# Retention's output product by seven block products over both halves of the contraction, with block sums made in DRAM by accumulating DMAs and the gate applied at the end

## The chip, the cores and the metric

The kernel runs on one core of one Trainium2 chip. The core has a matrix engine (TensorE, PE in the profile), three engines for elementwise work (VectorE or DVE, ScalarE or ACT, GpSimd or POOL), a queue engine that here only issues DMAs (SyncE or SP), and 16 DMA engines, shared by all queues. The metric is device time in microseconds (us), the median of several runs. Each engine executes its own instructions strictly in the order in which the program emits them; engines are tied together by semaphores alone.

## The reference, cut to what matters

One decoder block, 1024 tokens by 1024 channels, all in float32. The part in question ends the retention branch:

```python
ro = (ro * gn_g + gn_b)                        # normalized heads, (S, 2048)
ret_out = (silu(rg) * ro) @ w_ret_out          # (S, 2048) @ (2048, 1024)
...
att_out = att @ w_att_out                      # (S, 512) @ (512, 1024)
merged = sigmoid(gate_a) * ret_out + sigmoid(gate_b) * att_out
x = x + g1 * (merged @ w_o)
```

Call `u = silu(rg) * ro` the gated head output; `ret_out` is a product with a contraction of 2048.

## The kernel before, in words

Activations lie transposed, channels on the 128 partitions and the 1024 tokens in the free dimension. Full precision comes from splitting each operand into a rounded part ("high", type fp32r) and the remainder ("low"): ScalarE copies the high part, VectorE subtracts to get the low part, and `mm3` (L191 to L199) issues three matmuls for each product of a 128x128 weight block with 512 tokens: low weight by high data (L195), high by low (L197), high by high (L199). So 128x128 by 512 tokens costs three PE instructions everywhere.

The stages, in order of time: the startup (loads of `x`, of the adaLN weights `w_ada` and of the first value weights, L377 to L418 and `av_first`, L774), the attention values (`av_step`, L849), the queries, keys and gates by seven block products (`queries_keys`, L934, class `Blocks`, L214), four retention heads (`v_first` L605, `v_rest` L621, `chunk` L670), the attention pairs (`att_step` L1326, `cover_step` L1360, `gate_step` L1410), the two output products, `w_o` (`wo_step`, L1540), and the MLP (`ff1`, `ff2_blocks`, `ff2`, `ff2_last`).

Seven block products are Winograd's form of Strassen's scheme: a product split in 2x2 blocks is made by seven products of sums of blocks in place of eight. The kernel uses it already for queries, keys and gates, for the first MLP product and for a part of the second.

The order of work is written out by hand. `Steps` (L55 to L130) runs a list of steps; each has weights (and other tiles) to load into a ring of three buffers `raw`, which SP issues ahead, and a preparation (the split) that is emitted one or two steps before the body that uses it. A step marked `manual` calls `ahead` itself at the place where the next step's preparation is to be emitted.

Around the change:

- `u_final` (L661) ends a retention head: ScalarE scales and shifts a 128x1024 tile `on` (L665), VectorE multiplies it by the silu of the gate (L667), SP stores it as `u` in DRAM (L668). That of the last head is emitted inside the first attention step (L1344).
- `att_out_step` (L1468) makes 192 matmuls in four steps (tiles `ao` in PSUM) and multiplies the gate of the attention branch, kept in SBUF as `G[1, i]` (tag `g1`), by the result (L1483). It also loads the eight tiles of the retention gate (`gate_load(0, i)`, L1474).
- `ret_out_step` (L1486), 16 steps of 48 matmuls: for each head `h` and output pair `j`, four 128-row slices of `u` (split by `u_prep`, L1444) by the weights `w_ret_out`. VectorE multiplies each PSUM result by the gate (L1495), and GpSimd, or for the last head VectorE, adds it to `G[1, i]` (L1496). With the last head the sum is split into `mh` and `ml` (L1502, L1503), 128x512 tiles from a ring of 32 buffers with tag `mh`, the operand of `w_o`.
- `wo_step` makes two halves of 512 tokens by eight outputs, 24 matmuls each.

GpSimd's own order: one small power for the first norm (L356), eight DMAs near the end of `queries_keys` that bring back the second halves of the normalized input (L950, L951), small jobs in the retention heads (L561, L720), nothing in attention, the adds at L1496, and adds for the later norms (L1538).

Of the kernel before, what the change touches and what calls it, by code (L numbers as in the profile page):

```python
# [11 lines left out]
F32 = mybir.dt.float32  # L12
# [5 lines left out]
P = 128  # L18
D = 1024
S = 1024  # L20
# [34 lines left out]
class Steps:  # L55
# [16 lines left out]
    def run(self, pre):  # L72
# [42 lines left out]
        for s, (loads, body, manual) in enumerate(self.steps):  # L115
            prepare(s, len(loads))
            mine = weights_of(s)
            args = [r for r in results[s] if r is not None]
            if manual:
                body(lambda room=3 - mine, only=False: prepare(s + 1, room, only), *args)  # L120
            else:
                room = 3 - max(mine, 1)
                for t in (s + 1, s + 2):
                    if t < len(self.steps) and room > 0:
                        done = sum(getattr(p, "weight", False) for _, p in self.steps[t][0][:len(results[t])])
                        prepare(t, room - done, t == s + 2)
                        room -= weights_of(t)
                        if len(results[t]) < len(self.steps[t][0]):
                            break
                body(*args)  # L130

@with_exitstack
def block_kernel(ctx, tc, io, stop=None, dbg=None):
# [385 lines left out]
    u_d = [dram.tile([P, S], F32, name=f"u{i}") for i in range(16)]  # L519
# [141 lines left out]
    def u_final(h, es=range(4)):  # L661
        for e in es:
            i = h * 4 + e
            t = hd["on"][e]
            nc.scalar.activation(t, t, AF.Identity, scale=vec[:, VC_GNG + i:VC_GNG + i + 1],  # L665
                                 bias=vec[:, VC_GNB + i:VC_GNB + i + 1])
            nc.vector.tensor_mul(t, t, hd["srg"][e])  # L667
            nc.sync.dma_start(u_d[i], t)  # L668
# [265 lines left out]
    def queries_keys(ahead):  # L934
        sums_of_h("t4")
# [390 lines left out]
    def att_step(pair, i):  # L1326
# [3 lines left out]
        def body(*args):  # L1330
# [7 lines left out]
            elif pair == 0:  # L1338
# [5 lines left out]
                u_final(H - 1)  # L1344
                open_att()
# [98 lines left out]
    def u_prep(h, e):  # L1444
        def prep(raw):
            if h % 2 == 0:
                r = []
                for j in range(2):
                    s = raw[:, 512 * j:512 * j + 512]
                    hi, lo = mh(f"uh{h}{e}{j}"), mh(f"ul{h}{e}{j}")  # L1450
                    nc.scalar.copy(hi, s)
                    nc.vector.tensor_sub(lo, s, fv(hi))
                    r.append((hi, lo))
            else:
                hi = A["r1"].tile([P, S], F32R, tag="att", bufs=8, name=f"uh{h}{e}")
                lo = A["r1"].tile([P, S], F32R, tag="att", bufs=8, name=f"ul{h}{e}")
                nc.scalar.copy(hi, raw)
                nc.vector.tensor_sub(lo, raw, fv(hi))
                r = halves(hi, lo)
            G["u", h, e] = r  # L1460
        return prep

# [5 lines left out]
    def att_out_step(j):  # L1468
        def body(w):
            xs = [halves(*A["att", h]) for h in range(4)]  # L1470
            for i in (2 * j, 2 * j + 1):
                if j < 2:
                    gate_load(1, i + 4)
                gate_load(0, i)  # L1474
# [9 lines left out]
        return body  # L1484

    def ret_out_step(h, j):  # L1486
        def body(w):
            xs = [G["u", h, e] for e in range(4)]
            for f in range(2):
                i = 2 * j + f  # L1490
                ps = ps_mm(f"ro{h}{j}{f}")
                k4_mm(ps, w, f, xs)
                m, sg = G[1, i], G[0, i]
                t = G["mp"].tile([P, S], F32, tag="rl", bufs=2, name=f"rt{h}{i}")
                nc.vector.tensor_mul(t, flat(ps), sg)  # L1495
                (nc.vector if h == H - 1 else nc.gpsimd).tensor_add(m, m, t)  # L1496
                if h == H - 1:
                    r = []
                    for hf in range(2):
                        s = m[:, 512 * hf:512 * hf + 512]  # L1500
                        hi, lo = mh(f"mh{i}{hf}"), mh(f"ml{i}{hf}")
                        nc.scalar.copy(hi, s)  # L1502
                        nc.vector.tensor_sub(lo, s, fv(hi))  # L1503
                        r.append((hi, lo))
                    G["m", i] = r
            if h == H - 1 and j > 0:
                x1_load(2 * j - 2)
                x1_load(2 * j - 1)
        return body


    behind = []
    for j in range(4):
        steps.add(att_out_step(j), [wsplit(io["w_att_out"][j])] + behind)
        behind = [(u_d[j], u_prep(0, j))]
    for h in range(H):
        for j in range(4):
            steps.add(ret_out_step(h, j), [wsplit(io["w_ret_out"][4 * h + j])] + behind)
            behind = [(u_d[4 * (h + 1) + j], u_prep(h + 1, j))] if h + 1 < H else []
# [20 lines left out]
    def wo_step(hf, f):  # L1540
        def body(w):
            if hf == 0 and f == 0:
                x1_load(6)
                x1_load(7)
# [8 lines left out]
            for k in range(NK):  # L1553
                mm3([ps], wk(w, k), [G["m", k][hf]], k == 0, k == NK - 1)
# [128 lines left out]
    def ff1(ahead):  # L1683
# [7 lines left out]
        banks(True)  # L1691
# [383 lines left out]

def _vcols(w, width):
# [45 lines left out]
def pack(x, c, w_ada, b_ada, norm1_g, w_in, rel_bias, ret_gn_g, ret_gn_b,  # L2122
# [23 lines left out]
        "w_ret_out": _k4(A(w_ret_out)[0]),  # L2146
# [25 lines left out]
```

## Time and profile before

| | us |
|---|---|
| median of 3 runs | 2281.12 |
| lowest and highest run | 2278.60 and 2281.48 |
| the profiled execution, whole | 2279.53 |
| its span, first to last instruction | 2277.7 |
| PE busy within the span | 2223.6 (98%) |
| VectorE, ScalarE, GpSimd busy | 1444.6, 848.5, 171.4 |

The span of the profiled execution is 1.8 us shorter than its device time; the rest lies before the first and after the last instruction. The granted TensorE clock was 0.997. Rows of the profile give an engine, a source line, an operation, "written <- read" by the program's names, a count, and times. "Idle before" is the time in which the engine stood still ahead of an instruction, with what released it. PE's matmuls overlap in the pipe, so one matmul's duration is longer than the distance to the next.

### The profile page before, as it was taken

The numbers are of one execution on the slowest core, as the hardware profiler recorded it, in microseconds if no ns is written. First come the engines' busy times: TensorE is split into PE (matmuls) and PEld (weight loads), VectorE is DVE, ScalarE is ACT, GpSimd is POOL, SyncE is SP. The second block draws the span as 40 slices with busy tenths as digits, with TensorE's granted clock in tenths as the row PEclk, the third lists the DMA queues.
The fourth block names the chain that finished last, engine by engine and source line by source line (L and its number), as shares of the span: only waits on it lengthen the run. The fifth ranks groups of instructions, "written<-read, shape, count | busy, mean of one in ns | idle before, by whom it ended". The sixth has DMA issues, their size and how long they took to land.

```text
span 2277.7 us, 26769 instructions
## 1 busy us (share of the span) xinstructions
PE 2223.6 (98%) x10322; PEld 1837.4 (81%) x10322; DVE 1444.6 (63%) x2149; ACT 848.5 (37%) x1557; POOL 171.4 (8%) x136
## 2 busy tenths in 40 slices
PE   7999999999999999999999999999999999999998
PEld 5887888888878787888788788888777788788887
DVE  6526555546767687764554646666876665787845
ACT  4333233212334343344534522124454444433412
POOL 0000000001101020100000004501100000000003
PEclk9999999999999999999999999999999999999999
DMA  9533333333323223233323353335134443754322
GB/s 360 198 122 111 111 112 111 111 123 117 121 84 121 93 84 136 68 132 94 103 77 103 103 203 93 99 106 200 60 141 153 153 152 111 271 174 167 120 84 74
DMA packets 112317, 293.53 MB, mean 129 GB/s; under 512 B 23094, under 2 KB 34621, under 8 KB 112062
## 3 DMA queue, kind: packets, MB, share of 16 engines
q1 hardware_dynamic: 111038, 289.72, 36.7%
q0 software_dynamic: 1152, 2.10, 0.3%
q8 instruction: 81, 1.33, 0.2%
q14 instruction: 46, 0.38, 0.0%
HBM read 217.70 MB, written 76.44 MB: 129 GB/s over the span
## 4 chain that ended last, share of the span: by engine, by line
PE 45%; DVE 9%; ACT 4%; issue 2%; DMA 1%; POOL 0%; SPq 0%; POOLq 0%; DVEq 0%; ACTq 0%
PE ro L195 3%; PE ro L197 3%; PE ro L199 3%; PE fp L195 2%; PE fp L197 2%; PE fp L199 2%; PE ak L195 2%; PE ak L197 2%; PE ak L199 2%; PE f2a L197 2%; PE f2a L199 2%; PE f2a L195 2%; PE f2c L199 1%; PE f2c L195 1%; PE f2c L197 1%
## 5 line engine op out<-in xcount | busy, mean ns | idle before, releaser
L1496 POOL TENSOR_TENSOR g<-g,rt 128x1024 f32<-128x1024 f32 x24 | 66.1, 2754 | 431.3 <-DVE rt L1495 431.3
L195 PE MATMUL qap<-hh,qaw 128*128 128x512 f32 x216 | 84.3, 390 | 2.5 <-DVE qat L279 1.7
L199 PE MATMUL qap<-hh,qaw 128*128 128x512 f32 x216 | 84.1, 389 | 0.0
L197 PE MATMUL qap<-hl,qaw 128*128 128x512 f32 x216 | 84.0, 389 | 0.0
L1495 DVE TENSOR_TENSOR rt<-ro,g 128x1024 f32<-128x1024 f32 x32 | 39.0, 1219 | 56.4 <-PE ro L199 44.2
L561 POOL TENSOR_TENSOR j<-qk,j 128x512 fp32r<-128x512 f32 x32 | 43.8, 1370 | 364.4 <-ACT j L560 364.4
L1538 POOL TENSOR_TENSOR accnf<-accnf,sqnf 128x256 f32<-128x256 f32 (+1 forms) x18 | 16.6, 920 | 624.9 <-ACT sqnf L1537 624.9
L1640 ACT ACTIVATE a<-a 128x512 f32<-128x512 f32 x48 | 30.3, 632 | 84.9 <-DVE a L1639 84.9
L252 DVE TENSOR_TENSOR qaw<-wa,qaw 128x512 fp32r<-128x512 f32 x54 | 36.7, 690 | 39.5 <-ACT qaw L242 39.5
L1126 ACT ACTIVATE P<-P,ng 128x128 f32<-128x128 f32 (+1 forms) x96 | 41.9, 439 | 40.2 <-DVE ng L1123 40.2
L252 DVE TENSOR_TENSOR fw<-w1r,fw 128x512 fp32r<-128x512 f32 x48 | 33.0, 688 | 37.5 <-ACT fw L242 37.5
L639 ACT CAST vh<-v 128x512 fp32r<-128x512 f32 x32 | 18.8, 587 | 89.1 <-PE v L603 82.7
L1825 ACT CAST w2h<-w2s 128x512 fp32r<-128x512 f32 x36 | 22.4, 621 | 78.7 <-DVE w2s L1863 78.7
L581 ACT COPY sm<-sT 128x128 f32<-128x128 f32 x32 | 8.5, 266 | 114.1 <-PE sT L572 114.1
L195 PEld LDWEIGHTS qap<-hh,qaw 128*128 128x128 f32 x216 | 40.5, 188 | 11.7 <-DVE qat L279 2.1
L195 PE MATMUL fp<-h2h,fw 128*128 128x512 f32 x128 | 50.0, 390 | 0.0
L199 PE MATMUL fp<-h2h,fw 128*128 128x512 f32 x128 | 49.8, 389 | 0.0
L197 PE MATMUL fp<-h2l,fw 128*128 128x512 f32 x128 | 49.8, 389 | 0.0
L199 PEld LDWEIGHTS qap<-hh,qaw 128*128 128x128 f32 x216 | 40.5, 188 | 8.5
L197 PEld LDWEIGHTS qap<-hl,qaw 128*128 128x128 f32 x216 | 40.5, 188 | 8.3
L242 ACT CAST qaw<-wa 128x512 fp32r<-128x512 f32 x54 | 32.5, 617 | 36.0 <-PE qap L199 36.0
L278 DVE TENSOR_TENSOR qat<-qat,qap 128x512 f32<-128x512 f32 x18 | 12.4, 687 | 50.1 <-PE qap L199 50.1
(3202 smaller groups left out, 7192.6 us busy)
## 6 DMA issues: line engine op xcount, KB each, us to landing
raw<-in_w_ada_dram SPq DMA_DIRECT2D x32, 512.0 KB, 3.5
w1r<-in_w_ff_dram SPq DMA_DIRECT2D x32, 512.0 KB, 5.0
xsd<-as SPq DMA_DIRECT2D x24, 512.0 KB, 2.7
w2r<-in_w_ff2s_dram SPq DMA_DIRECT2D x24, 512.0 KB, 7.6
em<-in_w_ada_dram SPq DMA_DIRECT2D x16, 512.0 KB, 10.2
qkd<-qa SPq DMA_DIRECT2D x16, 512.0 KB, 2.6
raw<-in_w_rv_dram SPq DMA_DIRECT2D x16, 512.0 KB, 4.4
raw<-in_w_rg_dram SPq DMA_DIRECT2D x16, 512.0 KB, 3.6
```

Source lines behind the costliest of these rows:

```text
L195: nc.tensor.matmul(o, wl, xh, start=first, stop=False, skip_group_check=skip)
L197: nc.tensor.matmul(o, wh, xl, start=False, stop=False, skip_group_check=skip)
L199: nc.tensor.matmul(o, wh, xh, start=False, stop=last, skip_group_check=skip)
L242: nc.scalar.copy(t[:, :512], src)
L252: nc.vector.tensor_sub(t[:, 512:], src, fv(t[:, :512]))
L561: nc.gpsimd.tensor_sub(t[:, 1], src, fv(t[:, 0]))
L639: nc.scalar.copy(vh[c], ps)
L1126: nc.scalar.activation(v, v, AF.Exp, bias=ng[:, blk:blk + 1], accum_out=st[:, g, blk, 2 + a:3 + a])
L1495: nc.vector.tensor_mul(t, flat(ps), sg)
L1496: (nc.vector if h == H - 1 else nc.gpsimd).tensor_add(m, m, t)
L1640: nc.scalar.activation(o, o, AF.Relu)
L1825: nc.scalar.copy(hi, src)
```

## The change

The output product of retention is made by seven block products. The contraction of 2048 splits into alternating 128-row slices (slice index even or odd), the 1024 outputs likewise, and the tokens into two halves; each of the seven products has a contraction of 1024 (two steps of 512, so 14 steps in the list `RSEQ`), four output tiles and 512 tokens. The operands' block sums are made in DRAM: a plain DMA copies the first block, a second DMA adds the other to it, both issued by GpSimd.

```diff
@@ Steps.run
                 for t in (s + 1, s + 2):
+                    if t < len(self.steps) and self.steps[t][2] and not self.steps[t][0]:
+                        break
@@ after vtile
-    u_d = [dram.tile([P, S], F32, name=f"u{i}") for i in range(16)]
+    y_d = dram.tile([P, 4, 8, 512], F32, name="y")
+    yt_d = {n: dram.tile([P, 8, 512], F32, name=f"y{n}") for n in ("t1", "t2", "t3", "t4")}
+    YB = ("11", "12", "21", "22")
+    ws_d = {n: dram.tile([P, 4, 1024], F32, name=f"wro{n}") for n in ("11", "12", "22", "s1", "s2", "s3", "s4")}
+    def dma_sum(out, x, y):
+        flat = lambda t: t.rearrange("p a b -> p (a b)").rearrange("p (a b) -> p a b", b=2048)
+        nc.gpsimd.dma_start(flat(out), flat(x))
+        nc.gpsimd.dma_start(flat(out), flat(y), accum_op=ALU.add, max_dma_last_dim=8192)
+    def weight_sums():
+        b11, b12, b21, b22 = (io["w_ret_out"][i] for i in range(4))
+        dma_sum(ws_d["s1"], b21, b22)
+        dma_sum(ws_d["s3"], b21, b11)
+        dma_sum(ws_d["s2"], ws_d["s1"], b11)
+        dma_sum(ws_d["s4"], ws_d["s2"], b12)
+        for n, b in (("11", b11), ("12", b12), ("22", b22)):
+            nc.gpsimd.dma_start(ws_d[n], b)
+    def result_sums():
+        b11, b12, b21, b22 = (y_d[:, i] for i in range(4))
+        dma_sum(yt_d["t1"], b11, b12)
+        dma_sum(yt_d["t3"], b12, b22)
+        dma_sum(yt_d["t2"], yt_d["t1"], b22)
+        dma_sum(yt_d["t4"], yt_d["t2"], b21)
@@ u_final
-            nc.vector.tensor_mul(t, t, hd["srg"][e])
-            nc.sync.dma_start(u_d[i], t)
+            for hf in range(2):
+                b, g = t[:, 512 * hf:512 * hf + 512], hd["srg"][e][:, 512 * hf:512 * hf + 512]
+                if hf == i % 2:
+                    nc.vector.scalar_tensor_tensor(b, b, -1.0, g, op0=ALU.mult, op1=ALU.mult)
+                else:
+                    nc.vector.tensor_mul(b, b, g)
+            nc.sync.dma_start(y_d[:, 2 * (i % 2):2 * (i % 2) + 2, i // 2], t.rearrange("p (t x) -> p t x", t=2))
@@ queries_keys
     def queries_keys(ahead):
+        weight_sums()
@@ att_step, pair 0, first step
                 u_final(H - 1)
+                result_sums()
@@ u_prep and ret_out_step go; att_out_step
-                gate_load(0, i)
+            if j < 3:
+                r_x_load(j)
+            if j in (0, 3):
+                r_w_load(j // 3)
+            if j == 1:
+                r_x(0, 0)
+                r_x(0, 1)
+            elif j == 2:
+                r_w(0, 0)
+                r_w(0, 1)
+            elif j == 3:
+                r_x(1, 0)
+                r_x(1, 1)
+                r_flush()
@@ new
+    RPLAN = {"11": ("11", -1, "a"), "s1": ("t1", 1, "c"), "s2": ("t2", 1, "a"), "s4": ("22", 1, "c"),
+             "s3": ("t3", -1, "a"), "12": ("21", 1, "b"), "22": ("t4", -1, "a")}
+    RSEQ = [(n, c) for n in RPLAN for c in range(2)]
...
+    def r_x_load(i):
+        n, c = RSEQ[i]
+        b = RPLAN[n][0]
+        src = y_d[:, YB.index(b)] if b in YB else yt_d[b]
+        for m in range(4):
+            Q["x", i, m] = mh(f"rl{i}{m}")
+            nc.sync.dma_start(fv(Q["x", i, m]), src[:, 4 * c + m])
+    def r_x(i, j):
+        for m in (2 * j, 2 * j + 1):
+            lo, hi, sign = Q["x", i, m], mh(f"rh{i}{m}"), float(RPLAN[RSEQ[i][0]][1])
+            nc.scalar.activation(hi, fv(lo), AF.Copy, scale=sign)
+            r_low(lo, hi, sign)
+            Q["x", i, m] = hi, lo
+    def r_low(*now):
+        Q["last"].append(now)
+        if len(Q["last"]) > 1 or not now:
+            lo, hi, sign = Q["last"].pop(0)
+            if sign > 0:
+                nc.vector.tensor_sub(lo, fv(lo), fv(hi))
+            else:
+                nc.vector.scalar_tensor_tensor(lo, fv(lo), -1.0, fv(hi), op0=ALU.mult, op1=ALU.subtract)
+    def r_w_load(i):
+        n, c = RSEQ[i]
+        src = ws_d[n]
+        for s in range(2):
+            lo = r_place(i, "l", s)
+            nc.sync.dma_start(fv(lo), src[:, 2 * c + s])
+            Q["w", i, s] = lo
+    def r_place(i, part, s):
+        name = f"rw{part}{i}{s}"
+        if i == 0:
+            return G["p"].tile([P, 1024], F32R, tag="g0", bufs=8, name=name)
+        if i % 3 == 1:
+            return whl.tile([P, 1024], F32R, tag="w" + part, name=name)
+        return A["r1"].tile([P, 1024], F32R, tag="att", bufs=8, name=name)
+    def r_w(i, s):
+        lo, hi = Q["w", i, s], r_place(i, "h", s)
+        nc.scalar.copy(hi, fv(lo))
+        r_low(lo, hi, 1.0)
+        Q["w", i, s] = hi, lo
...
+    def r_mm(i, p):
+        n, c = RSEQ[i]
+        bank = RPLAN[n][2]
+        new = n in ("11", "s1", "12") and c == 0
+        if new and bank != "c":
+            Q["ps", bank, p] = ps_s(f"ro{bank}{p}")
+        hi, lo = Q["w", i, p // 2]
+        for m in range(4):
+            k = slice(512 * (p % 2) + m * P, 512 * (p % 2) + m * P + P)
+            mm3([Q["ps", bank, p]], (hi[:, k], lo[:, k]), [Q["x", i, m]], new and m == 0, m == 3, True)
+    def r_post(n, p):
+        ps = Q["ps", RPLAN[n][2], p]
+        if n == "11":
+            Q["r", 2 * p] = G["p"].tile([P, S], F32, tag="g0", bufs=8, name=f"ret{2 * p}")
+        if n == "s1":
+            Q["r", 2 * p + 1] = G["p"].tile([P, S], F32, tag="g0", bufs=8, name=f"ret{2 * p + 1}")
+        if n == "22":
+            return
+        e, o = Q["r", 2 * p], Q.get(("r", 2 * p + 1))
+        dst = {"11": e[:, :512], "12": e[:, :512], "s2": e[:, 512:], "s4": e[:, 512:]}.get(n)
+        if n[0] == "s" and n in ("s1", "s3"):
+            dst = o[:, 512:]
+        if n in ("11", "s1", "s2"):
+            nc.scalar.copy(dst, ps)
+        else:
+            (nc.vector.tensor_add if n == "12" else nc.vector.tensor_sub)(dst, dst, ps)
+    def r_gate_load(blk):
+        for j in range(2):
+            t = G["mp"].tile([P, 2, 512], F32, tag="rl", bufs=2, name=f"ga{blk}{j}")
+            for e in range(2):
+                hf = int(blk[1]) - 1
+                nc.sync.dma_start(t[:, e], gate_d[4 * j + 2 * e + int(blk[0]) - 1][:, 512 * hf:512 * hf + 512])
+            Q["ga", blk, j] = t
+    def r_final(blk, p):
+        i, hf = 2 * p + int(blk[0]) - 1, int(blk[1]) - 1
+        hs = slice(512 * hf, 512 * hf + 512)
+        m, ga = G[1, i][:, hs], Q["ga", blk, p // 2][:, p % 2]
+        if blk == "21":
+            nc.vector.scalar_tensor_tensor(ga, Q["ps", "a", p], -1.0, ga, op0=ALU.mult, op1=ALU.mult)
+        else:
+            nc.vector.tensor_mul(ga, ga, Q["r", i][:, hs])
+        nc.vector.tensor_add(m, m, ga)
+        if blk == "21":
+            t = A["r1"].tile([P, S], F32R, tag="att", bufs=8, name=f"m{i}{hf}")
+            hi, lo = t[:, :512], t[:, 512:]
+        else:
+            hi, lo = mh(f"mh{i}{hf}"), mh(f"ml{i}{hf}")
+        nc.scalar.copy(hi, m)
+        nc.vector.tensor_sub(lo, m, fv(hi))
+        G["m", i, hf] = hi, lo
+    DONE = {"s4": "12", "s3": "22", "12": "11"}
+    def ret_out(ahead):
+        banks(True)
+        for p in range(4):
+            Q["ps", "c", p] = ps_s(f"roc{p}")
+        for i, (n, c) in enumerate(RSEQ):
+            if i + 2 < len(RSEQ):
+                r_w_load(i + 2)
+            if i + 3 < len(RSEQ):
+                r_x_load(i + 3)
+            blk = {6: "12", 9: "22", 11: "11", 13: "21"}.get(i)
+            if blk:
+                r_gate_load(blk)
+            for p in range(4):
+                r_mm(i, p)
+                if Q["post"]:
+                    r_post(*Q["post"].pop())
+                if c == 1:
+                    Q["post"].append((n, p))
+                if p < 2 and i + 1 < len(RSEQ):
+                    r_w(i + 1, p)
+                elif p > 1 and i + 2 < len(RSEQ):
+                    r_x(i + 2, p - 2)
+                if p == 3 or i >= len(RSEQ) - 2:
+                    r_flush()
+                if c == 0 and i > 0 and RSEQ[i - 1][0] in DONE:
+                    r_final(DONE[RSEQ[i - 1][0]], p)
+                if i == len(RSEQ) - 1:
+                    if p == 1:
+                        ahead(1)
+                    if p > 0:
+                        r_final("21", p - 1)
+            if i == len(RSEQ) - 2:
+                for f in (1, 3, 5, 7):
+                    x1_load(f)
+        for f in (0, 2, 4, 6):
+            x1_load(f)
+        r_final("21", 3)
...
+    steps.add(ret_out, manual=True)
@@ wo_step
-            for k in range(NK):
-                mm3([ps], wk(w, k), [G["m", k][hf]], k == 0, k == NK - 1)
+            ks = (0, 2, 4, 6, 1, 3, 5, 7)
+            for k in ks:
+                mm3([ps], wk(w, k), [G["m", k, hf]], k == 0, k == 7)
@@ ff1: banks(True) goes (it is at the start of ret_out now)
```

`r_flush` does the subtractions that `r_low` still holds back. The weights are also laid out differently in DRAM on the host, in blocks of 128 partitions by 4096 numbers.

More of the change, by code (lines that the diff above doesn't have):

```diff
@@ L1442, in mh @@
         return G["mh"].tile([P, 512], F32R, tag="mh", bufs=32, name=name)
[L1444 to L1461, printed above, removed]
     def k4_mm(ps, w, f, xs, ks=range(4)):
@@ L1483, in body @@
                 nc.vector.tensor_mul(m, m, flat(ps))
-        return body
[L1486 to L1509, printed above, removed]
@@ L1522, in x1_load @@
+    for j in range(4):
+        steps.add(att_out_step(j), [wsplit(io["w_att_out"][j])])
+    steps.add(ret_out, manual=True)
     def x1_load(f, src=None):
```

24 lines of the change are left out of this document (12 added, 12 removed).

## The prediction

> **What bounds the kernel now.** I read the page's first part, then busy time by stretch, then the instructions of single engines in order of time. The busy row says that PE sets the time:
>
> ```profile
> span 2277.7 us, 26769 instructions
> PE 2223.6 (98%) x10322; PEld 1837.4 (81%) x10322; DVE 1444.6 (63%) x2149; ACT 848.5 (37%) x1557; POOL 171.4 (8%) x136
> ```
>
> The stage that is replaced is the stretch from 1356 to 1530 us; beside it the attention stage and three pieces of the startup (columns: stretch, length, then busy time and count of PE, PEld, DVE, ACT, POOL; clock, DMA share, GB/s):
>
> ```profile
> 1356.00:1530.00 174.00, 174.00 (x769) 144.09 (x768) 111.96 (x85) 35.41 (x45) 66.09 (x24) 1.00 0.31 102
> 1020.00:1312.00 292.00, 281.89 (x1569) 240.62 (x1569) 162.48 (x259) 144.06 (x340) 0.00 (x0) 1.00 0.30 94
> 19.20:54.00 34.80, 31.90 (x131) 25.09 (x132) 31.06 (x47) 11.33 (x13) 0.03 (x1) 1.00 0.99 394
> 54.00:170.00 116.00, 115.45 (x509) 95.27 (x508) 51.35 (x74) 39.33 (x60) 0.00 (x0) 1.00 0.46 159
> 20.00:30.00 10.00, 9.69 (x39) 7.33 (x37) 7.52 (x11) 4.40 (x6) 0.00 (x0) 1.00 1.03 410
> ```
>
> In the retention product PE has no gap: 768 matmuls in 174.0 us, one each 0.2266 us, at full clock. VectorE, GpSimd and the DMAs are covered there, so only the number of matmuls counts. The startup differs: from 19 to 54 us the DMA engines are full (0.99), and VectorE is nearly full too (31.06 of 34.8).
>
> **The change, part by part.**
>
> *Matmuls.* Before, 16 steps of 48 = 768; after, 14 of 48 = 672, of the same shape. 96 x 0.2266 = **-21.8 us**, if PE stays gapless.
>
> *What leaves.* 24 GpSimd adds, 32 gate products of VectorE and the `u` splits: all lie under PE's 174 us, so they give nothing. `u_final` gets two 512-wide products for one of 1024 (16 x 0.16 us at the durations below), which PE's attention and value matmuls cover. The eight gate loads become 16 of half the size, later; `banks(True)` moves to a place where PE is gapless, and the one product it follows is drained while the first bank is filled: nothing.
>
> *Elementwise work in the new stage.* The nearest rows (mean ns after the busy time):
>
> ```profile
> L1503 DVE TENSOR_TENSOR ml<-g,mh 128x512 fp32r<-128x512 f32 x16 | 10.4, 689 | 5.5 <-ACT mh L1502 5.5
> L1502 ACT CAST mh<-g 128x512 fp32r<-128x512 f32 x16 | 9.1, 619 | 34.1 <-DVE g L1496 34.1
> L1458 DVE TENSOR_TENSOR ul<-raw,uh 128x1024 fp32r<-128x1024 f32 x8 | 9.7, 1216 | 0.0
> L1457 ACT CAST uh<-raw 128x1024 fp32r<-128x1024 f32 x8 | 8.4, 1049 | 10.6 <-PE ao L197 5.3 <-PE ro L197 5.3
> L1562 DVE SCALAR_TENSOR_TENSOR x<-wo,mods,x 128x512 f32<-128x512 f32 x16 | 11.9, 745 | 6.8 <-PE wo L199 6.8
> ```
>
> Steps are counted from 0 to 13, as in `RSEQ`. One lasts 48 x 0.2266 = 10.88 us on PE and asks of VectorE two weight splits (2 x 1.22) and four data splits (4 x 0.69): 5.2 us, and of ScalarE 4.6. That fits until step 7. From step 8 on `r_final` adds 4 x (0.69 + 0.69 + 0.69) us, with VectorE waiting 0.62 us for ScalarE in each: 10.8. And it needs buffers: the ring `mh` has 32. In step i it holds both parts of steps i and i+1 (16), the raw tiles of i+2 and i+3 (8), and takes the high parts of i+2 (4): 28. Each finished block keeps 8 until `w_o`. So in step 10 (block "12" kept, "22" being made) the ring is full, and ScalarE's copy stands until a tile pair of step 10's own data is free. That is in its last quarter: 3 x 2.72 + 0.68 = 8.84 us after its start. Behind that copy, in the order of ScalarE and VectorE, stand the weight splits of the next step. With 0 at step 10's start:
>
> - copy to 9.5, its low part 10.2, low part of step 11's first weights 11.4; due at 10.88: PE waits 0.5.
> - the next two finals and step 12's first data splits follow, 11.4 to 18.6; the third data split needs a tile of step 11 (11.4 + 8.84 = 20.3); then the last final (24.9), one sum from PSUM (25.6), step 12's first weights (26.9). Due at 22.3: PE waits 4.6.
> - block "11" in step 12 waits the same way (26.9 + 8.84); VectorE is through with it at 46.4, with the `w_o` weights at 48.0. PE ends step 13 at 48.7, but the four finals of block "21", 2.75 each, last until 59.0. The first `w_o` product has 24 matmuls and could end at 54.1; it ends at 59.5: 5.4 late; the next one's weights come 1.2 after that.
>
> Sum **+11.8 us**. Bounds: 0, if tiles come free in another order than I count; and about 18, if they come free only at a step's end (three waits each 2.04 later).
>
> *Loads of the new stage.* 14 x 2 MB, 4 MB of gates and 4 MB of `x` in some 152 us: 237 GB/s, against 410 in the startup row. Each is asked for a step (10.9 us) ahead of its split; the same tensors' loads land in 2.9 to 5.9 us (below). Hidden.
>
> *Sums of the results.* POOL has nothing else in attention (0.00 above). The rows for its start, its deadline and its company:
>
> ```profile
> 1004.23 3.73 SPq L668 DMA_DIRECT2D u<-on  x4
> 1333.74 0.41 PEld L195 LDWEIGHTS ao<-ah,raw_10162l 128*128 128x128 f32 x2
> SPq L1185 <- DMA std<-st: 8.6, 4, 3.3
> u<-on SPq DMA_DIRECT2D x16, 512.0 KB, 2.9
> g<-gated SPq DMA_DIRECT2D x15, 512.0 KB, 5.9
> em<-in_w_ada_dram SPq DMA_DIRECT2D x16, 512.0 KB, 10.2
> ```
>
> It starts when the last head's stores (issued until 1008) have landed, 2.9 us later; the first sum is loaded with the third step of the attention's output product, 1334. Eight transfers would have to take 40 us each to be late. Until then they share the DMA engines with attention's loads (share 0.30). What could hurt is the small round trip through DRAM for which SP stands 3.3 us at worst, with the next key weights queued behind; those are read a step later, and the 48 matmuls of a step last 10.9 us. I take 0, bounds 0 and 5.
>
> *Sums of the weights.* The call stands at the head of `queries_keys`, but GpSimd runs in its own order, and these DMAs read only inputs. What GpSimd does before:
>
> ```profile
> 16.66 2.57 POOL L356 TENSOR_TENSOR n1rs<-n1rs,ct 128x8 f32<-128x8 f32 x1 [16.21 <-DVE n1rs L355]
> 500.94 0.74 POOL L950 DMA_DIRECT2D hh<-h12d  x1 [481.72 <-PE qap L199]
> ```
>
> Nothing from 19.2 to 500.9 us. So the eleven transfers of 2 MB **begin at 19.2 us, in the middle of the saturated startup**, not at 160. What the startup waits for:
>
> ```profile
> 52.11 1.06 ACT L768 CAST raw_490h<-raw 128x1024 fp32r<-128x1024 f32 x1 [2.58 <-DMA raw<-in_w_av_dram]
> ...
> 52.35 1.28 DVE L462 SCALAR_TENSOR_TENSOR xt<-xt,a,rb 128x1024 f32<-128x1024 f32 x1
> 53.55 1.22 DVE L769 TENSOR_TENSOR raw_490l<-raw,raw_490h 128x1024 fp32r<-128x1024 f32 x1
> 54.85 1.28 DVE L467 SCALAR_TENSOR_TENSOR hl<-xt,mods,hh 128x1024 fp32r<-128x1024 f32 x1
> ...
> 61.31 0.50 PE L756 MATMUL av<-raw_490l,hh 128*128 128x512 f32 x1 [0.55 <-ACT hh L464]
> ```
>
> ScalarE waits 2.58 us for the load of `raw_490` until 52.1; VectorE takes its low part at 53.55 without a gap before or after; PE's next group waits for that chain. Behind L769 stand VectorE's scalings of the last channel tiles, so a later load moves the whole chain, with a slack of 0.4 us. From 19.2 to 52.1 the loads need 32.9 us of full DMA engines. How much longer with the sums beside them, no row shows. Below: 0, if the loads are served first. Above: the work of all sums, 7 copies of 2 MB at 410 GB/s (5.1 us) and 4 additions, estimated at twice that since two streams are read: 77 us. I take equal shares, nearest to the saturated row, in which the loads queue up (10.2 us to land against 2.9 for a lone store of the size). A copy then takes 10.2 us, an addition 20.5, each followed by 2.9 us until it has landed and GpSimd can issue the dependent one; of these 36.5 us the loads get 5.1 + 10.2 + 5.8 = 21.1, or 0.58. 32.9 / 0.58 = 56.9: **+24 us**. Behind it the queue has room (0.46 of share from 54 to 170 us): nothing more.
>
> The Trainium skill, "DMA: Bandwidth & Descriptors", section "Queues, rings and completion order", speaks against this change: a DMA engine takes turns between the queue rows that have work, a whole packet from each. The sums' rows are 8 KB long and the loads' 4 KB; if a row is a packet, that means a third for the loads. No run here shows two loaded queues yet. The second rival prices it.
>
> *Sum.* 2279.5 (the profiled execution) - 21.8 + 11.8 + 24 = **2293.5 us**. The median before, 2281.1, is 1.6 above that execution.
>
> **Rivals.**
>
> 1. *Startup unharmed, faster than before.* If the sums take little from the loads (or begin after them), the +24 goes: 2269.5, and with the buffer stalls gone too 2257.7. It decides at a delay of 24 - 9 = 15 us, where the loads get 0.69. For it: 0.4 us is the slack of one load only, and GpSimd's waits leave the queue free between sums. Against it: the row at 0.99 has no room for 2 MB.
> 2. *The loads get a third.* Copy 7.7 us, addition 15.4, waits 5.8: of 28.9 us the loads get 13.5, or 0.467; 32.9 / 0.467 = 70.4, a delay of 37.5: 2307.0. For it: longer rows in the sums. Slower additions than I estimate lead the same way, up to 2346 at the upper bound.
> 3. *The ring is no limit*, the stalls of 11.8 vanish: 2281.7, the same as before. For it: my count is by hand. Against it: 44 tiles wanted of 32.
> 4. *GpSimd is late at 501 us.* The sums' chain has 482 us for 11 transfers; beyond 43 us for each, the reload of the input waits, and PE with it. Against it: 2.9 us for a quarter of the size.
>
> **How the numbers follow.** Forecast 0.42, first rival 0.20, second 0.22, third 0.10, fourth and worse 0.06. The forecast's own range is 2285 to 2304 (delay of 16 to 35). For 8 in 10 I reach down into the first rival, 2268, and up past the second, 2318. A difference of 0.2% (4.6 us) is about what a measurement of this kernel can tell from none. Faster by more: the first rival and a little of the third, 0.21. Within it: most of the third and the forecast's edge, 0.12. Slower: 0.67.
>
> **What would show it.** After: 672 matmuls of the product, 0.2266 us apart except ahead of steps 11 and 12; PE idle some 5 us in the first `w_o` product, released by VectorE at the split of block "21"; GpSimd's first DMA near 19 us; queue q0 with some 40 MB (19 transfers of 2 MB beside the 2 MB of before); `raw_490` split near 77 us and the first `qap` matmul some 24 us late. Wrong would be a first DMA of GpSimd behind 60 us, or a startup that ends on time though q0 is busy, or a gapless product.

## The result, and the profile after

The changed kernel takes **2339.3 us** (median; 2338.2 to 2341.0), the kernel before 2281.3 (2278.6 to 2281.7): a ratio of 1.026, interval 1.024 to 1.028. Forecast were 2293.5 us, with a range up to 2318. The sign was right; the time lies 46 us above the forecast and outside the range.

Two lines of the page of the changed kernel answer to the busy row of before:

```profile
span 2336.4 us, 26856 instructions
PE 2218.6 (95%) x10226; PEld 1827.3 (78%) x10226; DVE 1432.8 (61%) x2213; ACT 880.1 (38%) x1613; POOL 119.5 (5%) x131
```

The 96 matmuls are gone (10322 to 10226), but the span is 58.7 us longer: PE's share fell from 98% to 95%. Where, the start of the first matmul of each stage tells (us, from the instructions of PE by tile; the two kernels on the right are experiments told below):

| first matmul of | before | after | after - before | e5, sums late | e9, and splits later |
|---|---|---|---|---|---|
| queries and keys (qap) | 159.4 | 220.2 | +60.8 | 159.5 | 160.2 |
| heads (v) | 505.2 | 566.4 | +61.2 | 506.1 | 506.7 |
| attention (ak) | 995.0 | 1058.4 | +63.4 | 998.1 | 999.7 |
| retention product (ro, roa) | 1355.7 | 1420.9 | +65.2 | 1359.6 | 1360.8 |
| first feed-forward product (fp) | 1618.7 | 1677.1 | +58.4 | 1615.3 | 1603.7 |
| second, its first part (f2a) | 1945.7 | 2003.2 | +57.5 | 1942.3 | 1930.0 |
| span's end | 2277.7 | 2336.4 | +58.7 | 2277.3 | 2263.2 |

So the startup loses 60.8 us, heads and attention some 4 more, and product and `w_o` together gain 6.8 of the 21.8. After that nothing of size happens. GpSimd in order of time shows the cause of the first number, as forecast to the microsecond at its start (in brackets: idle time before, and what ended it):

```profile
16.72 2.56 POOL L358 TENSOR_TENSOR n1rs<-n1rs,ct 128x8 f32<-128x8 f32 x1 [16.27 <-DVE n1rs L357]
19.23 0.72 POOL L532 DMA_DIRECT2D wros<-in_w_ret_out_dram  x1
30.22 0.92 POOL L533 DMA_DIRECT2D wros<-in_w_ret_out_dram  x1 [10.27 <-DMA wros<-in_w_ret_out_dram]
30.81 0.83 POOL L532 DMA_DIRECT2D wros<-in_w_ret_out_dram  x1
54.12 0.91 POOL L533 DMA_DIRECT2D wros<-in_w_ret_out_dram  x1 [22.47 <-DMA wros<-in_w_ret_out_dram]
...
105.85 1.82 POOL L542 DMA_DIRECT2D wro<-in_w_ret_out_dram  x3
```

L532 is a copy, L533 the addition on top of it. After the first addition (30.22) the next sum's copy follows 0.6 us later: it depends on nothing. From there **two** transfers are under way. ScalarE's split of the load that the forecast followed (raw_486 here, raw_490 before):

```profile
97.49 1.04 ACT L804 CAST raw_486h<-raw 128x1024 fp32r<-128x1024 f32 x1 [33.12 <-DMA raw<-in_w_av_dram]
```

Before it stood at 52.11, the forecast had it near 77: 45.4 us late instead of 24. The DMA queues by stretch (19 to 30, 30 to 54, 54 to 77, 77 to 97, 97 to 130 us; columns: packets, MB, share of the engines' time; q0 carries the sums, q1 the loads and stores):

```profile
q1 hardware_dynamic: 650, 2.36, 54.1%
q0 software_dynamic: 48, 2.10, 47.3%
...
q0 software_dynamic: 320, 4.19, 63.2%
q1 hardware_dynamic: 990, 3.60, 39.0%
...
q0 software_dynamic: 320, 4.19, 66.1%
q1 hardware_dynamic: 878, 3.20, 36.4%
...
q1 hardware_dynamic: 1117, 4.06, 52.6%
q0 software_dynamic: 272, 2.10, 50.3%
...
q0 software_dynamic: 400, 8.39, 84.4%
q1 hardware_dynamic: 587, 1.47, 14.6%
```

The loads get 0.53 to 0.54 in the stretches with one transfer, but 0.36 to 0.39 in those with two. Added up to 97 us: 0.541 x 11 + 0.390 x 24 + 0.364 x 23 + 0.526 x 20 = 34.2 us of full engines; the forecast asked for 32.9. The sum closes: this share is the delay.

These stretches mix two states, since between the last packet of one transfer and the first of the next the loads have the engines to themselves. Cut where the packets of q0 begin and end, the same rows read as follows (23.1 to 29 us, the first copy alone; 34.4 to 53.2, an addition and a copy together; 81.8 to 94.6, an addition alone):

```profile
q0 software_dynamic: 47, 2.10, 88.1%
q1 hardware_dynamic: 74, 0.26, 12.1%
...
q0 software_dynamic: 319, 4.19, 80.7%
q1 hardware_dynamic: 419, 1.53, 21.4%
...
q0 software_dynamic: 270, 2.10, 78.6%
q1 hardware_dynamic: 337, 1.21, 24.9%
```

While the sums move, the loads get only 0.12 beside the copy, 0.25 beside the addition and 0.21 beside both; in the gaps, such as 29 to 34.4 us, they have all of the engines. Together a copy and an addition take 18.8 us, as long as the two alone (5.9 and 12.8). So what two at once cost the loads is one of the gaps of some 5 us.

The remaining 15.4 us arise behind it. SP in order of time, changed kernel, then the kernel before:

```profile
100.20 4.00 SPq L431 DMA_DIRECT2D browd<-rows  x1
106.45 2.83 SPq L434 DMA_DIRECT2D biasd<-browd  x4
109.33 0.56 SPq L431 DMA_DIRECT2D browd<-rows  x1
140.79 2.39 SPq L434 DMA_DIRECT2D biasd<-browd  x4
143.23 0.55 SPq L431 DMA_DIRECT2D browd<-onehot  x1
147.93 2.39 SPq L434 DMA_DIRECT2D biasd<-browd  x4
150.83 0.36 SPq L85 DMA_DIRECT2D raw<-in_w_av_dram  x1
```

```profile
55.18 0.39 SPq L429 DMA_DIRECT2D browd<-rows  x1
...
74.28 0.36 SPq L85 DMA_DIRECT2D raw<-in_w_av_dram  x1
```

Three small stores of the bias rows go to DRAM and are loaded again; SP stands until each has landed. Before, that took 19.1 us, now 50.6, since one store alone needs 31.5 us (109.3 to 140.8) behind the last addition and the three copies. The next weights are asked for 50 us after the first store, and PE waits.

In the new stage the waits of PE (1420 to 1600 us: who, on whom, total, times, longest) are nearly those of the forecast:

```profile
PE roa L197 <- DVE rwl L1550: 4.3, 1, 4.3
PE wo L197 <- ACT m L1638: 3.0, 3, 1.2
PE wo L199 <- DVE m L1639: 0.5, 2, 0.2
PE rob L197 <- DVE rwl L1550: 0.4, 1, 0.4
PE wo L197 <- DVE raw_10509l L188: 0.3, 1, 0.3
```

0.4 us ahead of step 11 (forecast 0.5), 4.3 ahead of step 12 (4.6), then 3.8 in gaps of the first products with `w_o`. The clock adds to them (changed kernel by stretch; the clock is the column after POOL):

```profile
80.00:90.00 10.00, 0.00 (x0) 0.00 (x0) 0.25 (x1) 0.00 (x0) 0.00 (x0) 0.50 1.05 286
160.00:170.00 10.00, 10.00 (x35) 8.04 (x35) 6.77 (x10) 3.83 (x6) 0.00 (x0) 0.77 1.02 405
1500.00:1540.00 40.00, 40.00 (x178) 33.10 (x178) 29.31 (x42) 12.04 (x18) 0.00 (x0) 1.00 0.60 197
1557.00:1562.00 5.00, 5.00 (x17) 3.96 (x16) 5.00 (x9) 1.99 (x4) 0.00 (x0) 0.66 0.97 380
```

Behind the 4.3 us gap PE is busy without a break, yet does 17 matmuls in 5 us instead of 22; the granted clock is 0.66.

### The profile page after: what moved, and what is told of

It is laid out like the page before. It is cut to its first block, busy times and chain, and to the rows that moved or that the text cites. A ratio compares the mean times of both kernels' runs of the same rounds, so it can differ in the third digit from the quotient of the medians.

```text
span 2336.4 us, 26856 instructions
## 1 busy us (share of the span) xinstructions
PE 2218.6 (95%) x10226; PEld 1827.3 (78%) x10226; DVE 1432.8 (61%) x2213; ACT 880.1 (38%) x1613; POOL 119.5 (5%) x131
## 4 chain that ended last, share of the span: by engine, by line
PE 43%; DVE 9%; ACT 4%; DMA 2%; issue 2%; SPq 0%; POOL 0%; POOLq 0%; DVEq 0%; ACTq 0%
PE fp L197 2%; PE fp L199 2%; PE fp L201 2%; PE f2a L199 2%; PE f2a L201 2%; PE f2a L197 2%; PE ak L197 1%; PE ak L199 1%; PE ak L201 1%; PE wo L197 1%; PE wo L201 1%; PE wo L199 1%; PE roa L197 1%; PE roa L199 1%; PE roa L201 1%
## 5 line engine op out<-in xcount | busy, mean ns | idle before, releaser
L254 DVE TENSOR_TENSOR fw<-w1r,fw 128x512 fp32r<-128x512 f32 x48 | 33.0, 688 | 37.5 <-ACT fw L244 37.5
L197 PE MATMUL roa<-rh,rwl 128*128 128x512 f32 x128 | 50.6, 396 | 4.3 <-DVE rwl L1550 4.3
L670 ACT CAST vh<-v 128x512 fp32r<-128x512 f32 x32 | 18.8, 589 | 89.9 <-PE v L634 87.8
L199 PE MATMUL roa<-rl,rwh 128*128 128x512 f32 x128 | 50.4, 394 | 0.0
L201 PE MATMUL roa<-rh,rwh 128*128 128x512 f32 x128 | 50.4, 394 | 0.0
L1550 DVE TENSOR_TENSOR rwl<-rwl,rwh 128x1024 fp32r<-128x1024 f32 x26 | 31.4, 1221 | 25.5 <-ACT rwh L1581 25.5
```

The costliest lines, as they stand in the source:

```text
L197: nc.tensor.matmul(o, wl, xh, start=first, stop=False, skip_group_check=skip)
L199: nc.tensor.matmul(o, wh, xl, start=False, stop=False, skip_group_check=skip)
L201: nc.tensor.matmul(o, wh, xh, start=False, stop=last, skip_group_check=skip)
L254: nc.vector.tensor_sub(t[:, 512:], src, fv(t[:, :512]))
L670: nc.scalar.copy(vh[c], ps)
L1550: nc.vector.tensor_sub(lo, fv(lo), fv(hi))
```

## The experiments

Theory: the sums' transfers beside the startup's loads cost the 60.8 us, the full ring `mh` some 14 us, and the saved matmuls are worth their 21.8. Rival: the transfers cost their work wherever they run, and the gaps of the stage have another cause.

**e1, the sums held until the startup is over.**

```
-        weight_sums()
         sums_of_h("t4")
+        gate = cst.tile([P, 1], F32, name="gate")
+        nc.gpsimd.tensor_copy(gate, fv(XA["t4", 3][0])[:, :1])
+        weight_sums()
```

> The changed kernel, with the eleven transfers of the weight sums held on GpSimd behind one small copy that reads the last operand sum of the queries and keys, so that they begin when the startup is over, near 165 us. Theory: the 60.8 us by which the first qap matmul came late are all due to the sums' transfers beside the startup's loads; there is room for them in the queries and keys. The first qap matmul is back near 159.4 us and the time is 2339.3 - 60.8 = 2278.5 us, within 4. Rival: the transfers' work has to be paid wherever they run, since the loads of queries and keys slow down beside them: the startup ends on time, but gaps ahead of qap matmuls give back 20 us or more, 2300 to 2339 us.

2294.1 us, ratio to before 1.006 (1.004 to 1.008): between theory and rival. The first qap matmul is back at 159.1, so the startup's loss is the sums'; but 15.6 us more than expected are missing. Queries and keys last 352.1 us instead of the changed kernel's 346.2, with gaps of 6.6 us against 2.9; the rest lies above all in matmuls that last 0.396 us instead of 0.389 late in the kernel (e5, e11).

**e2, the kernel before with the eleven transfers and nothing else** (`weight_sums()` at the head of `queries_keys`, outputs unread).

> The kernel before, with nothing changed but that GpSimd also issues the same eleven transfers (seven copies, four accumulating ones) at the same place; nobody reads what they write. Theory: they alone make the startup's loss: 2281.3 + 60.8 = 2342 us, first qap matmul near 220 us. Rival: part of the 60.8 us comes from the rest of the change (its other code and DRAM tensors); then less than 50 us are lost here, under 2331 us.

2340.0 us, ratio 1.026 (1.024 to 1.027), first qap matmul at 219.8. The transfers alone make the whole loss; the rest of the change takes and gives about the same.

**e3, only the three plain copies held.** The diff of e1, but the gate stands ahead of the copies alone.

> The changed kernel, with only the three plain copies, the last of the eleven transfers, held until the startup is over; the eight transfers of the four sums still begin at 19 us. Theory: the startup has two losses. The first, 45.4 us until the split of raw_486, is that of the sums; the second, the rest of the 60.8 us, comes from the three copies, issued together at 105 us, behind which the small round trip of the bias rows takes 32 us while SP stands. Without the copies 15.4 us come back: 2324 us, and the round trip is short. Rival: the round trip is long behind any two loaded queues, and the last sum or the loads that pile up are enough for it: 2339 us, within 4.

The first qap matmul comes at 204.8: exactly 15.4 us earlier, and SP gets past the bias rows in 30.4 us (99.39 to 129.78). The time, 2335.7 us (ratio 1.024, 1.022 to 1.025), does not show it, since this kernel too has the added 4-byte tile and its 0.396 us matmuls. By the stage the theory holds, by the time alone it would have fallen.

**e4, the splits of blocks 12 and 22 moved out of the stage**, sums as in the change (the first edit in `r_final`, the second in `wo_step`, for its first half and `f < 4`).

```
+        elif hf == 1:
+            return
...
+                for i in ((1, 0), (2, 3), (4, 5), (6, 7))[f]:
+                    m, h, l = G[1, i][:, 512:], mh(f"mh{i}1"), mh(f"ml{i}1")
+                    nc.scalar.copy(h, m)
+                    nc.vector.tensor_sub(l, m, fv(h))
+                    G["m", i, 1] = h, l
```

> The changed kernel, with the sums where they are (in the startup), but the splits of the finished blocks 12 and 22 moved out of the new stage into the first four products with w_o, which do not read these blocks: 16 of the 24 ring buffers that finished blocks keep are asked for only when the stage is over. Theory: the full ring makes the gaps ahead of steps 11 and 12 (0.4 and 4.27 us) and, through VectorE's lateness, the gaps in the first w_o product (some 6 us) with the slow clock behind them (some 3 us): without it the stage is gapless, and 2339.3 - 14 = 2325 us. Rival: the ring is no limit, and the gaps come from elsewhere (loads of the stage, VectorE's sums from PSUM): they stay, 2336 to 2341 us.

2324.1 us, 15.2 less than the change. All waits of PE from the product's start to 1590 us:

```profile
PE wo L197 <- DVE raw_10509l L188: 0.7, 1, 0.7
PE wo L199 <- DVE m L1641: 0.2, 1, 0.2
```

Of the 15.2, 4.2 stand at the first qap matmul (216.0 instead of 220.2) and are not the edit's; from the product's start to fp it is 242.8 us (1417.5 to 1660.3) instead of 256.2: **13.4 us** for the stage.

**e5, e1 with a spare column in place of the new tile.**

```
-    ng2 = cst.tile([P, 2 * NK], F32, name="ng2")[:, :NK]
+    ng2 = cst.tile([P, 2 * NK], F32, name="ng2")
+    spare, ng2 = ng2[:, NK:NK + 1], ng2[:, :NK]
```

> The same as with the sums held until the startup is over (2294.1 us there), but the small copy that holds them writes a spare column of a tile that is there anyway, so that no tile of SBUF is moved by 4 bytes. In that run the matmuls from the attention's output product on stood 0.396 us in the records where the changed kernel has 0.389, and the second feed-forward product took 235.9 us instead of 231.3. Theory: that is the shifted layout; here they are back at 0.389, and what is left of the sums' cost is the 6.6 us of gaps in the queries and keys: 2339.3 - 60.8 + 6.6 = 2285 us. Rival: the sums beside the queries and keys, or a lower clock, do it: 2292 to 2296 us again.

2279.5 us, ratio 0.9995 (0.9986 to 1.0004): no difference from before that can be measured, and 59.8 us less than the change. The gaps in queries and keys are 3.2 us here.

**e6, one transfer at the end of each chunk of the heads**, from 560 us on (`weight_sums` as a generator that yields behind each transfer; the second edit ends `chunk`).

```
-        dma_sum(ws_d["s1"], b21, b22)
...
+            yield
...
         hd["o", c] = on
+        next(Q["ws"], None)
```

> The changed kernel, with the eleven transfers of the weight sums issued one by one, each at the end of a chunk of the retention heads (some 28 us apart, from 570 us on), in an order in which a transfer's source is done one chunk or more before. Theory: the sums cost something only where loads have no slack or where several are under way at once; here nothing: first qap matmul at 159, no gap in queries and keys, heads and attention as in the changed kernel: 2339.3 - 60.8 = 2278.5 us, the same as before within 0.2%. Rival: the heads' loads, with VectorE and PE both busy there, wait beside each transfer as the queries and keys did: 0.5 to 2 us for each, 2284 to 2300 us.

2291.0 us, ratio 1.005 (1.003 to 1.006): the rival. My spacing was wrong: a chunk lasts some 9.5 us, not 28, so eight transfers went out from 560.3 to 627.3, nearly back to back, and the heads took 503.9 us (505.9 to 1009.8) instead of the 492.0 of e5. Most of it is one wait for the weights of the next head:

```profile
PE v L635 <- ACT raw_4498vh L586: 8.2, 1, 8.2
```

**e7, e6 and e4 together.**

> Both: the weight sums spread over the retention heads, and the splits of blocks 12 and 22 moved into the first products with w_o. Theory: the saved matmuls (21.8 us) come through when neither the startup nor the ring takes them back: 2339.3 - 60.8 - 15.3 (measured for the later splits in the changed kernel) = 2263 us, 0.8% faster than before. Rival: the later splits gave 15.3 us only because the startup was disturbed in another way in that run (first qap matmul at 216.0 instead of 220.2); then they are worth 11 here: 2267.5 us.

2277.0 us, ratio 0.998 (0.997 to 0.999). Dearer than expected by e6's loss; the later splits are worth 14.0 beside e6.

**e8, the sums in 4 KB rows.**

```
+        if out.shape[1] == 4:
+            for z, op in ((x, ALU.bypass), (y, ALU.add)):
+                for j in (0, 2):
+                    nc.gpsimd.dma_start(out[:, j:j + 2], z[:, j:j + 2], accum_op=op, max_dma_last_dim=4096)
+            return
...
-            nc.gpsimd.dma_start(ws_d[n], b)
+            for j in (0, 2):
+                nc.gpsimd.dma_start(ws_d[n][:, j:j + 2], b[:, j:j + 2], max_dma_last_dim=4096)
```

> The changed kernel, with the transfers of the weight sums in the startup cut into 4 KB rows instead of 8 KB (and each transfer given as two of 1 MB); same bytes, same place. Theory by turns: DMA engines take turns between the queues by packets that hold a row or two, so shorter rows give the loads a larger share: raw_486 is split near 80 us instead of 97.5, and the time is 2320 us or less. Rival: the share does not hang on the length of the rows: raw_486 near 97, 2335 to 2342 us.

2313.8 us, ratio 1.015 (1.014 to 1.017): the theory. The split of raw_486 comes at 76.78. The queues from 19 to 30 us, and from 46.5 to 72.5 us, where the sums move without a break:

```profile
q1 hardware_dynamic: 894, 3.26, 73.5%
q0 software_dynamic: 338, 1.32, 29.2%
...
q0 software_dynamic: 1073, 4.19, 60.0%
q1 hardware_dynamic: 1241, 4.52, 44.2%
```

Over the first stretch the loads get 0.74 where they got 0.54. In the second, beside copies and additions that move, they get 0.44; the change had 0.21 there. The edit also cuts each transfer in two, and GpSimd stands up to 12 us at an issue, so that the number under way differs too. But in the change the loads' share was as low beside one addition (0.25) as beside two transfers (0.21), which leaves the rows' length; no run changes it alone.

**e9, the version that the runs point to: e5 with e4.**

> The version that the runs point to: the weight sums held until the startup is over (small copy into the spare column), and the splits of blocks 12 and 22 moved into the first products with w_o. Theory: the gains add: 2279.5 (sums late) - 14.0 (later splits, 2291.0 to 2277.0 with the sums in the heads) = 2265.5 us, 0.6 to 0.7% faster than before. Rival: with both, the loads that the sums delay meet the stage, or the later splits delay the loads of the feed-forward weights: 2272 us or more.

2267.5 us, **ratio 0.994 (0.993 to 0.996)**: it beats both kernels. From the product's start to fp it takes 242.9 us instead of 263.0 before: 20.1 of the 21.8 us have come through.

**e10, the ring with 34 buffers** (sums as in e5; `bufs=32` to 34).

> The kernel with the sums late (2279.5 us), and the ring mh with 34 buffers instead of 32; all work stays as it was, the splits too. The runs with later splits took work from VectorE and ScalarE as well as buffers from the ring; this one takes nothing but the lack of two buffers. Theory, ring: the finals' copies stand for a shorter time, the gap ahead of step 12 (4.27 us) falls below 3 us, and the time by 2 to 6 us: 2274 to 2277.5. Rival: VectorE's work in steps 8 to 13 makes the gaps, and buffers do not matter: within 1.5 us of 2279.5.

2275.9 us, ratio 0.998 (0.997 to 0.999), 3.6 less than e5. The two longest waits of its stage:

```profile
PE wo L198 <- ACT m L1640: 2.5, 2, 1.3
PE roa L198 <- DVE rwl L1552: 0.9, 1, 0.9
```

Two buffers more, and the gap ahead of step 12 falls from 4.3 to 0.9 us. There it is the ring. The gaps in the first products with `w_o` stay at 3.5 us, as in e5; e4 removed most of them, but it moved work of VectorE and ScalarE as well as buffers, so for these the two are not told apart.

**e11, a 4-byte tile in the kernel before.**

```
+    shift = cst.tile([P, 1], F32, name="shift")
+    nc.gpsimd.memset(shift, 0.0)
```

> The kernel before, with one more tile of 4 bytes in each partition among the constants, filled once by GpSimd and never read; every tile that is laid out behind it moves by 4 bytes. Theory: the layout alone makes the 0.396 us matmuls seen where a 4-byte tile was added: some 10 to 15 us lost, 2290 to 2296 us, with 0.396 in the feed-forward products. Rival: the shift costs nothing by itself, and the two runs with it were slower for another reason: 2278 to 2283 us.

2292.5 us, ratio 1.005 (1.004 to 1.007): the layout alone costs 12 us. A group of the second feed-forward product, before and here (min, median, max ns; first and last start):

```profile
L195 PE MATMUL f2a<-b00h,w2l x8: 389/389/389, 1945.7 to 1954.5; 128*128 128x512 f32 x8
```

```profile
L197 PE MATMUL f2a<-b00h,w2l x8: 395/396/397, 1951.5 to 1960.6; 128*128 128x512 f32 x8
```

**e12, the sum s3 last, so that one transfer at a time is under way.**

```
-        dma_sum(ws_d["s3"], b21, b11)
         dma_sum(ws_d["s2"], ws_d["s1"], b11)
         dma_sum(ws_d["s4"], ws_d["s2"], b12)
+        dma_sum(ws_d["s3"], b21, b11)
```

> The changed kernel with one line moved: the sum s3, which depends on no other sum, comes last instead of second, so that until the third sum is done each transfer waits for the one before and only one is under way at a time; same transfers, same rows, same start. Theory: the loads' share falls with the number of transfers under way: 0.53 to 0.54 with one (a copy or an addition), 0.36 to 0.39 with two, by the changed kernel's stretches. With one at a time raw_486 needs 32.9 / 0.53 = 62 us and is split near 81 us instead of 97.5; the first qap matmul comes 10 to 17 us earlier than 220.2, 2322 to 2330 us. Rival: the share hangs on the additions or on the loads' own state in these stretches, not on the number: raw_486 near 97 us, 2336 to 2342 us.

A miss by the time: 2337.0 us (ratio 1.025, 1.023 to 1.027). Its first half came, in part: raw_486 is split at 87.34, 10.2 us earlier than in the change and 6 later than expected. The queues from 34.3 to 47.5 us, where an addition moves alone, and from 52 to 57.8, where a copy does:

```profile
q0 software_dynamic: 269, 2.10, 76.2%
q1 hardware_dynamic: 369, 1.34, 26.6%
...
q0 software_dynamic: 40, 2.10, 88.9%
q1 hardware_dynamic: 71, 0.26, 11.7%
```

The loads get 0.27 beside the addition and 0.12 beside the copy, as in the change, and all of the engines in the gaps of 4.5 to 5.4 us behind each. So the number under way does not set the share, as the theory had it: one behind the other there are more gaps, and they account for the 10.2 us. The gain went in the second half: SP passes the bias rows from 90.05 to 146.36 us here, 56.3 us, so the first qap matmul comes only 3.8 us earlier (216.4).

**e13, the round trips of the bias rows moved behind the startup**, every transfer of the sums left in place (from `av_first` to the head of `queries_keys`).

```
-                if k == 4:
-                    for g in range(3):
-                        bias_out(g)
...
+        for g in range(3):
+            bias_out(g)
```

> The changed kernel, with the sums where they are, but the three round trips of the bias rows through DRAM (each a store, for which SP stands, and four loads) issued at the start of the queries and keys instead of in the startup. Theory: SP stands behind them for 50 us (19 before), and that is the second loss: without them the next load is issued near 100 us instead of 150.8, the first qap matmul comes some 15 us earlier than 220.2, and the time is 2324 us, within 4. Rival: beside the last copies the loads have 15% of the engines, and a load asked for earlier lands no earlier than the copies end, near 140: at most 5 us come back, 2334 to 2341 us. A result between 2328 and 2334 means both.

2330.2 us, ratio 1.023 (1.020 to 1.025), so "both" by the expectation. The stage says more: the split of raw_486 is unmoved (96.91), and the first qap matmul comes at 204.9, **15.3 us earlier**. The second loss is SP's standing. Queries and keys then take 351.6 us (204.9 to 556.5) instead of 346.2: 5.4 us are given back, 5.1 of them in new gaps there.

## Why the prediction was wrong, point by point

- *Matmuls, -21.8.* Right: 96 fewer, and 20.1 us come through in e9.
- *The ring, +11.8.* The mechanism and its two gaps in the stage were right (e4, e10). Its size was 13 to 15: product and `w_o` gained 6.8 instead of 21.8 us in the change, and e4 gives back 13.4. The gaps alone were smaller than forecast (0.4 + 4.3 + 3.8 = 8.5 us, those in `w_o` 3.8 instead of 6.6); what was missing is the lower clock behind them.
- *Loads of the new stage hidden.* Right: no load is waited for there (e4).
- *Sums of the results, 0 with a bound of 5; `u_final`, nothing.* Attention up to the product became 1.8 us longer, inside the bounds, the heads 2.2 us. No run takes either alone.
- *Sums of the weights, +24 with bounds of 0 and 77.* **This step failed.** That the transfers start at 19.2 us and that they alone do the harm was right (e1, e2). So was their work: the first copy took 47.3% of 11 us = 5.2 us of full engines (estimated 5.1), and the 4.19 MB of the next stretch, a copy and an addition, 15.2, so an addition takes 10.0 (10.2). Three parts of it were wrong:
  - "I take equal shares" gave the loads half while a transfer moves and, with waits of 2.9 us between the transfers, 0.58 over all. While the sums moved, the loads got 0.12 beside a copy and 0.23 to 0.27 beside an addition (change, e12); that the gaps lasted some 5 us made up for a part. Chained one behind the other, as I had them on paper, the transfers delay the load by 35.2 us (e12: 87.34 against 52.11), not 24.
  - The code does not chain them so. The copy of the second sum depends on nothing, so GpSimd issued it beside the first addition, two transfers went out together, and a gap was missing for each pair. The delay of raw_486 was 45.4 us.
  - "Behind it the queue has room: nothing more" looked only at the share of before (0.46). What lay behind was not bandwidth but SP, standing for three small stores that now land behind 2 MB copies: 15.4 us (e3, e13).
- *The second rival*, a third for the loads: 37.5 us, nearer than the forecast, and close to the 35.2 us of e12, which chains the transfers as its sum did. That is in part luck: the loads got less than a third, and the gaps were longer than 2.9 us. The Trainium skill, "DMA: Bandwidth & Descriptors", section "Queues, rings and completion order", has the engines take turns by whole packets. The trace agrees with turns: for each packet of the sums 1.1 to 1.6 packets of the loads went, whatever its size (74 beside 47 of the copy, 337 beside 270 of the addition, 1241 beside 1073 in 4 KB rows, e8). But the figure of a third does not hold here, since the copy did not move in 8 KB packets: from 23 to 28 us 32 of them carry 2.10 MB, 64 KB each. An addition's carry 8 KB, and each takes the engines twice as long as a copy of the same size.

## What to carry to other kernels

A DMA on an engine's own queue starts when that engine's earlier instructions and its data allow it, not where the call stands; ask what else is on the DMA engines at that time, how large the packets of the new transfers are beside those of the loads, and how many of them depend on nothing and go out together. A share that is averaged over a stretch hides this; cut the stretch where the transfers begin and end. Then look for the small round trips: a queue that stands for a store to land pays the latency behind every large transfer, which no mean share shows. And when an edit that should only move work costs 10 us, compare the duration of one unchanged matmul first: a tile of 4 bytes was enough.

## What the runs showed of the hardware that was not expected

- A tile of 4 bytes ahead of the others lengthens the matmuls of some stages from 0.389 to 0.396 us, and the kernel before by 12 us (e11); the spare column instead of the tile gives 14.6 us back, a part of it in queries and keys, which last 346.6 instead of 352.1 us (e1, e5).
- Where PE had stood idle for some us, the granted clock was lower in this kernel: 0.50 in the long wait of the startup (80 to 90 us), and 0.66 in the 5 us behind the gap of 4.3 us.
- While transfers between DRAM tensors moved on the other queue, loads in 4 KB packets got 0.12 of the DMA engines beside a copy in 64 KB packets, 0.23 to 0.27 beside an addition in 8 KB packets, and 0.44 beside both in 4 KB packets (change, e12, e8).
- An accumulating transfer between DRAM tensors takes twice a copy's time of the DMA engines (10.0 against 5.2 us for 2 MB).
